# A third dense PSUM bank in the feed-forward part, three block sums and the samples' gating on GpSimd, and a recorder that knows the port shared with VectorE

## The chip, the cores and the metric

The kernel runs on one core of a Trainium2 chip. The core has a matrix engine (TensorE, PE in the profile), three engines for elementwise work (VectorE or DVE, ScalarE or ACT, GpSimd or POOL) and SyncE (SP), which here only starts transfers. They share an on-chip memory (SBUF); PE writes into eight banks of PSUM, which VectorE and ScalarE empty. The metric is the device time of one launch in microseconds (us), as the median over several runs.

## The reference

One layer of a decoder step for a prompt of 512 tokens and 8 x 4 sample tokens, which share all weights. D_MODEL is 1024, D_FF is 2816, everything is float32. The mixer and the cross attention come first; the part that the change touches is the feed-forward part and the last norm:

```
u = rmsnorm(x, norm_ffn)
ug = u @ w_gate
up = jnp.concatenate([conv_buf.astype(ug.dtype), ug], axis=1)
conv = conv_b + sum(conv_w[j] * up[:, j:j + T] for j in range(CONV_W))
x = x + (jax.nn.silu(conv) * (u @ w_up)) @ w_down
...
yp = rmsnorm(yp, norm_final)
ys = rmsnorm(ys, norm_final)
```

The prompt and the samples are two groups with conv states of their own; the kernel keeps their 512 + 32 = 544 tokens side by side as the columns of one matrix.

## The kernel before, in words

**Tiles.** Activations are kept transposed: 128 features on the partitions, 544 tokens along the row. D_MODEL is 8 such tiles (KT), D_FF is 22 (FT). A bank of PSUM holds 512 float32 numbers of a row, so every product is made in two halves of the tokens (CUTS: 256 and 288, LAST_CUTS: 288 and 256).

**Three products for one.** A float32 operand is split into a high part (rounded by a ScalarE cast to the fast matmul type) and a low part (what is left, a VectorE subtraction). A product is then high x high, high x low and low x high, three matmuls for each block of 128 x 128. Names that end in `h` and `l` are such parts: `wh` and `wl` of plain weights, `whg`, `wlg`, `whu`, `wlu` of gate and up weights, `wd_0h` and so on of down weights, `h16h` and `h16l` of hidden tile 16.

**The feed-forward part.** Tiles 0 to 3 of gate (`g`) and up (`u`) are plain products (`plain_tile`): 24 matmuls a half, into banks of the kind "dense" (`PD`, two of them). From tile 4 on, two tiles of one kind are made together by `Pair`, with a scheme that needs seven block products instead of eight. Its left factors are sums of weight blocks (A11, A12, S1 to S4, A22; S1 and S3 come from an accumulating transfer that GpSimd issues, S2 and S4 from VectorE). Its right factors are sums of blocks of the normed tokens: B11, B21, U, X, T, B22, V. These are made once, in `blocks(0)` and `blocks(1)`, each [128, 2, 272]: `norm` makes B11, B21, B12, B22 on VectorE, `combine` makes X = B12 - B22, T = B11 - B12, U = X - B11, V = B21 + U, `high` casts each, and `low` subtracts. The products of a pair go to three banks of the kind "aux" (`PX`, five): `ps_a`, `ps_d`, `ps_c`, followed by `g` or `u`. A unit is one pair of one kind; units 0 to 17 alternate gate and up for tiles 4, 6, ... 20.

**From gate and up to a hidden tile.** `conv` makes the three taps of the gate (ScalarE, then two VectorE operations, then Silu on ScalarE: `cv`) and copies the last columns away on GpSimd (`last`). `gated` multiplies up by it: `product` for the 512 prompt tokens on GpSimd, `product_s` for the 32 sample tokens on VectorE, then `high` and `low` split the result into `h..h` and `h..l`.

**Down.** The hidden tiles are taken in groups (DOWNS: 0 to 4, 4 to 8, 8 to 12, 12 to 16, 16 to 18), each 8 output tiles x 2 halves = 16 halves, 12 matmuls a half in a group of four blocks and 6 in the group of two. An entry says from which unit on the halves of a group may be placed, and how many go to each of the four places of a unit. Their bank is dense too (`ps_d`), and VectorE adds it to the residual `xr`. What is left goes behind the last unit. Tiles 18 to 21 (DOWN_LAST) make the last sixteen halves, `ps_dz`: first all eight tiles of the first tokens, then those of the others. Their weights are split into `wdhz` and `wdlz`.

**The end.** `final(c)` sums the squares over the features with two matmuls, makes 1/rms with Ln and Exp on ScalarE, and multiplies the residual by it and by the gain into `y`, on VectorE or (ON_POOL) on GpSimd, and sends it out. For the first half of tokens, ScalarE loads its table for Ln and Exp there, and the factor `r_fin` is in SBUF; for the second half VectorE reads it from a PSUM bank (`r_final`).

**The order of the work.** Nothing is issued as it is written. `Tape` records every operation as a `Step` with its engine, its estimated length, its tiles and what it depends on; `_Engine.take` holds the estimates. `order` then plays the five queues against each other with those lengths, takes for each free engine the ready step that is due first (`begin`), and issues in that order. It is a static order: on the chip every engine works its own queue strictly in it, and semaphores hold it where an input is late. `due` sets `begin` back from the matmuls that need a result; AHEAD says how many of the main PE steps before its own place a step may start at the earliest; `lead` and LEAD say how long before it is due. The profile calls nearly every instruction by the helper's line (606 for compute, 585 for a transfer), so it is read by the names of the tiles.

Of the kernel before, what the change touches and what calls it, by code (L numbers as in the profile page):

```python
# [10 lines left out]
F32 = mybir.dt.float32  # L11
F32R = mybir.dt.float32r
AF = mybir.ActivationFunctionType
# [20 lines left out]

PLAIN = 4

DOWNS = ((0, 4, 0, (1, 1, 1, 0)), (4, 8, 5, (1, 1, 1, 1)), (8, 12, 9, (1, 1, 1, 1)), (12, 16, 13, (1, 1, 1, 1)),
         (16, 18, 15, (1, 1, 1, 1)))
DOWN_LAST = (18, FT)
HT = N // 2  # L40
# [195 lines left out]
class Step:  # L236


    def __init__(self, engine, number, main):
        self.engine, self.number, self.main = engine, number, main  # L240
        self.calls, self.length, self.lag, self.bytes = [], 0.0, 0.2, 0
        self.deps, self.users, self.tiles = set(), [], set()
        self.gate, self.lead, self.after = None, None, set()

# [5 lines left out]
class Tape:  # L250
# [39 lines left out]
        dims = tuple(tuple(d) for d in ap.ap)  # L290
        return name, p0, p0 + dims[0][1], _bits(dims[1:]) << f0

    def put(self, engine, call, outs, ins, length, lag=None, size=0):
# [20 lines left out]
        cur.bytes += size  # L314
        if lag is not None:
            cur.lag = lag
        for ap, write in [(a, False) for a in ins] + [(a, True) for a in outs]:
            at = self.area(ap)
            if at is None:
                continue  # L320
            name, p0, p1, bits = at
            cur.tiles.add(name)
            kind = self.kinds.get(name)
            if kind in ("wraw", "whi", "wlo") and name not in self.seen:
                if kind in self.last:
                    cur.after.add(self.last[kind])
                self.last[kind] = cur
            found, keep = self.seen.setdefault(name, []), []
            for other in found:
                step, w, q0, q1, have = other  # L330
                if step is not cur and (write or w) and q0 < p1 and p0 < q1 and have & bits:
                    cur.deps.add(step)
                if not (write and p0 <= q0 and q1 <= p1 and have | bits == bits):
                    keep.append(other)
            keep.append((cur, write, p0, p1, bits))
            self.seen[name] = keep
            if write and engine == "PE":
                if name in self.writer and self.writer[name] is not cur:
                    cur.deps.add(self.writer[name])
                self.writer[name] = cur  # L340
        return None
# [40 lines left out]
    def due(self):  # L382

        for s in self.steps:
# [5 lines left out]
            if s.main:  # L390
                s.begin = s.est
            else:
                s.begin = s.soon + (self.SLACK if s.lead is None else 100.0)
                if s.engine in ("DVE", "ACT") and any(d.main for d in s.deps) and any(
                        self.kinds.get(n) in ("dense", "aux") for n in s.tiles):
                    s.begin = max(d.est + d.length for d in s.deps if d.main) + 1.0
            for d in s.deps:
                d.users.append(s)
# [24 lines left out]
    def order(self):  # L423
# [51 lines left out]
        def start(s):  # L475
# [11 lines left out]
                bus = max(bus, now) + s.bytes / 300e3  # L487
                s.end = bus + 2.0
            else:
                free[s.engine] = s.end = now + s.length  # L490
            if s.main:
                clock[:] = s.est, now
            for n in s.tiles:
# [23 lines left out]
        while todo:  # L517
# [4 lines left out]
            for e in ("SP", "ACT", "DVE", "POOL"):  # L522
                if free[e] <= now + 1e-9:
                    at = clock[0] + min(now - clock[1], 4.0)
                    can = [s for s in waiting[e] if s.ready <= now + 1e-9 and s.begin <= at + (s.lead or self.LEAD) and fits(s)]
                    if can:
                        start(min(can, key=lambda s: (s.begin, s.number)))
                        moved = True
            if free["PE"] <= now + 1e-9:
                can = [s for s in waiting["PE"] if s.ready <= now + 1e-9 and fits(s)]  # L530
# [34 lines left out]
class _Engine:  # L565
# [5 lines left out]
    def __getattr__(self, method):  # L571
# [3 lines left out]
        def take(*args, **kw):  # L575
# [6 lines left out]
            lag, size = 0.25, 0  # L582
            if method == "dma_start":
                size = 4 * int(np.prod(outs[0].shape))
                return tape.put(engine, lambda: call(*args, **kw), outs, ins, 0.1, 0.3, size)
# [15 lines left out]
            elif engine == "DVE":  # L601
                length = 0.13 + 0.00052 * n if method in ("tensor_scalar", "reciprocal") else 0.08 + 0.00105 * n
                length += 0.08 * ("accum_out" in kw)
            else:
                length = 0.15 + (0.0024 if method == "tensor_tensor" else 0.0009) * n
            return tape.put(engine, lambda: call(*args, **kw), outs, ins, length, lag, size)  # L606
        return take


# [1 line left out]
def tile_decoder_step(ctx: ExitStack, tc: tile.TileContext, xT, memT, kwT, vw, s0, conv_in, mkT, mv, vecs, cst,  # L611
# [23 lines left out]

    def PX(name):
        return tape.tile(psum, [128, 512], F32, tag="aux", name=name, bufs=5)

    def PDEC(name):
        return tape.tile(psum, [128, 512], F32, tag="dec", name=name, bufs=1)  # L640
# [1052 lines left out]

    dense_by_half(co_hl, KT, "co", co_evac, co_after)
    r_ffn, ux = ffn_in.r, ffn_in.hl
    tape.AHEAD = {"SP": 24, "ACT": 14, "DVE": 14, "POOL": 14, "PE": 14}
    ws.advance()
    ffn_in.rows(1)

# [47 lines left out]
    def conv(j, deps):  # L1747
# [13 lines left out]
                                               op0=ALU.mult, op1=ALU.add)  # L1761

        def gate():
            nc.scalar.activation(hid[j][:, :W], hid[j][:, :W], AF.Silu)

        job(ends, *deps)
        return job(gate, job(taps, job(first, *deps)))
# [1 line left out]
    def gated(j, deps):  # L1769
# [4 lines left out]

        def product_s():
            up, c = ups[j], hid[j]
            nc.vector.tensor_tensor(by_batch(up[:, SEQ:N]), by_batch(up[:, SEQ:N]), seg(c)[:, :, 0:4], op=ALU.mult)

        def high():
            hid[j] = R(f"h{j}h"), R(f"h{j}l")  # L1780
# [42 lines left out]
    def plain_half(w, xs, name, cut):  # L1823
# [2 lines left out]
        box = {}  # L1826

        def products():
            box["ps"] = PD(f"ps_{name}_{n0}")
            ws_, xs_ = w(), xs()  # L1830
            passes(box["ps"], ws_, xs_, n0, n, range(len(xs_)))

# [46 lines left out]


    tok, tok_low = {}, {}

    def blocks(kp):

# [12 lines left out]
                                               op0=ALU.mult, op1=ALU.mult)  # L1897

        def combine(name, a, b, op):
            nc.vector.tensor_tensor(place(name), tok[a, kp]["t"], tok[b, kp]["t"], op=op)  # L1900

        def split(name, part):
            tile = A if name in ("B11", "B21") or (name, part) == ("B22", "h") else B
# [4 lines left out]
            nc.scalar.copy(split(name, "h"), tok[name, kp]["t"])  # L1908

        def low(name):  # L1910
            nc.vector.tensor_tensor(split(name, "l"), tok[name, kp]["t"], tok[name, kp]["h"].bitcast(F32),
                                    op=ALU.subtract)

        for name in ("B12", "B22", "B11", "B21"):
# [164 lines left out]
    def last_half(m, c):  # L2079
        n0, n = LAST_CUTS[c]  # L2080
        cut = slice(n0, n0 + n)
        if m == 0 and c == 1:
            tape.gate_at = len(tape.mains) - 1
            nc.sync.dma_start(conv_out, last2)
            tape.gate_at = None
        ps = PD(f"ps_dz{m}_{c}")
        with tape.main():
            passes(ps, held[m], hs, n0, n, range(k))
        add_to(m)(ps, n0, n)
# [7 lines left out]
    def final(c):  # L2097
# [2 lines left out]
        ps = PX(f"psr_final{c}")  # L2100
        for i, sq in enumerate((ssq3.acc, last_sq)):
            nc.tensor.matmul(ps[:, :n], C("ones"), sq[:, cut], start=i == 0, stop=i == 1)
        with tape.together():
            if not c:
                nc.scalar.preload_act_table_set(LN_SET)
            nc.scalar.activation(r_fin[:, cut], ps[:, :n], AF.Ln, bias=eps, scale=1.0 / D)
        r = r_fin[:, cut]
        if c:

            r = PX("r_final")[:, :n]  # L2110
            nc.scalar.activation(r, r_fin[:, cut], AF.Exp, scale=-0.5)
# [99 lines left out]
```

## Time and profile before

| what | value |
| --- | --- |
| median of 3 runs | 842.91 us (842.23 to 843.27) |
| the profiled execution | 841.47 us |
| its span (first to last instruction) | 839.7 us |
| clock granted to TensorE, mean | 0.998 |
| TensorE busy | 821.3 us, 98% |
| VectorE busy | 592.0 us, 70% |
| ScalarE busy | 395.3 us, 47% |
| GpSimd busy | 182.9 us, 22% |

In the profile a row of a timeline gives the start, the length, the engine, the line, the operation, output <- inputs, the shape, and in brackets how long the engine had been idle and what ended that. A row of a group gives the count, the busy time, the mean of one in ns, and the idle time before the group's instructions. In a row of a stretch stand its bounds, its length, the busy time of PE, of PE's weight loads, of DVE, ACT and POOL with their instruction counts, the granted clock, the share of the DMA engines and GB/s. In a row by tile stand the shortest, middle and longest of the group in ns, and the first and last start.

The feed-forward part begins at about 450 us with the plain tiles; unit 0 begins at 500, the last product of a pair ends at 791, the `ps_dz` halves run from 804 to 831, and the last `y` is sent out at 836.

### The profile page before, as it was taken

To read this page: it belongs to the slowest core of one execution; us is meant where nothing else is said; L and a number is where in the kernel's file an instruction comes from. 1 tells how busy PE (TensorE), PEld (TensorE's weight loads), DVE (VectorE), ACT (ScalarE), POOL (GpSimd) and SP (SyncE) were. 2 spreads that over 40 slices of the span, in tenths; PEclk is the share of its full clock that TensorE was granted. 3 is DMA by queue.
4 is the path that set the end of the run, shared out by engine and by line. 5 is a ranking of instruction groups with operands and counts; after the bars stand their busy time and mean duration, and the time that the engine had idled before them with its cause. 6 is when DMAs were issued, how large, how long until landed. Compare 5 with 4: busy or idle time off the path is not lost.

```text
span 839.7 us, 18801 instructions
## 1 busy us (share of the span) xinstructions
PE 821.3 (98%) x7594; PEld 765.3 (91%) x7594; DVE 592.0 (70%) x1233; ACT 395.3 (47%) x792; POOL 182.9 (22%) x261
## 2 busy tenths in 40 slices
PE   9999999999999999999999999999999999999995
PEld 8989887878789879999789999999999999999995
DVE  6883725865888876564566997877877867767854
ACT  7422414543557454443445545555454545534623
POOL 1220000210210110222233252223213223232123
PEclk9999999999999999999999999999999999999999
DMA  9656895956833525161631246547455554564403
GB/s 321 221 140 191 260 334 190 301 168 221 291 111 104 181 82 179 59 216 36 223 113 51 76 124 155 139 123 193 132 124 141 157 148 124 156 161 115 134 1 107
DMA packets 90759, 132.32 MB, mean 158 GB/s; under 512 B 6064, under 2 KB 60080, under 8 KB 90544
## 3 DMA queue, kind: packets, MB, share of 16 engines
q1 hardware_dynamic: 84480, 120.69, 45.0%
q0 software_dynamic: 5184, 9.44, 7.0%
q8 instruction: 59, 0.97, 0.5%
q10 hardware_dynamic: 1008, 0.99, 0.3%
q14 instruction: 28, 0.23, 0.1%
HBM read 123.03 MB, written 8.07 MB: 156 GB/s over the span
## 4 chain that ended last, share of the span: by engine, by line
PE 84%; DVE 10%; issue 2%; DMA 1%; ACT 1%; POOL 1%; SPq 0%; DVEq 0%; POOLq 0%
PE ps_d L606 12%; PE ps_au L606 6%; PE ps_ag L606 6%; PE ps_wo L606 6%; PE ps_cg L606 3%; PE ps_cu L606 3%; PE ps_co L606 3%; PE ps_k L606 3%; PE ps_cq L606 3%; PE ps_hf L606 2%; PE ps_hq L606 2%; PE ps_v L606 2%; PE ps_hv L606 2%; PE ps_hg L606 2%; PE ps_dz L606 2%; PE ps_first L606 2%
## 5 line engine op out<-in xcount | busy, mean ns | idle before, releaser
L606 ACT CAST wh<-wr 128x1024 fp32r<-128x1024 f32 (+1 forms) x68 | 60.9, 908 | 109.3 <-PE ps_k L606 16.9
L606 DVE TENSOR_TENSOR wl<-wr,wh 128x1024 fp32r<-128x1024 f32 (+1 forms) x68 | 72.4, 1073 | 11.8 <-ACT wh L606 11.6
L606 POOL TENSOR_TENSOR up<-up,cv 128x512 f32<-128x512 f32 x22 | 34.1, 1552 | 165.0 <-ACT up L606 101.1
L606 POOL TENSOR_TENSOR hG<-hG,hf 128x256 f32<-128x256 f32 (+1 forms) x28 | 25.1, 895 | 189.0 <-DVE hf L606 127.8
L606 DVE TENSOR_TENSOR xr<-xr,ps_d 128x256 f32<-128x256 f32 x80 | 34.6, 433 | 23.8 <-PE ps_d L606 23.8
L606 DVE SCALAR_TENSOR_TENSOR cv<-ug,vec,cv 128x560 f32<-128x560 f32 x44 | 38.2, 868 | 0.2
L606 POOL COPY last<-ug 128x2 f32<-128x2 f32 (+1 forms) x44 | 19.9, 481 | 77.6 <-ACT ug L606 49.5
L606 POOL TENSOR_TENSOR acc_cx<-acc_cx,sq_cx 128x256 f32<-128x256 f32 (+1 forms) x14 | 11.9, 854 | 61.1 <-ACT sq_cx L606 61.0
L606 ACT ACTIVATE cv<-cv 128x560 f32<-128x560 f32 x22 | 14.8, 673 | 20.7 <-DVE cv L606 20.4
L606 PE MATMUL ps_co<-coh,wh 128*128 128x256 f32 (+1 forms) x64 | 19.0, 297 | 0.0
L606 ACT ACTIVATE cv<-ug,vec 128x560 f32<-128x560 f32 x22 | 18.8, 856 | 0.0
L606 ACT ACTIVATE P<-P,mx 128x128 f32<-128x128 f32 (+3 forms) x32 | 17.6, 551 | 2.7 <-DVE mx L606 2.7
L606 PE MATMUL ps_co<-coh,wl 128*128 128x256 f32 (+1 forms) x64 | 18.5, 288 | 0.0
L606 PE MATMUL ps_co<-col,wh 128*128 128x256 f32 (+1 forms) x64 | 18.4, 288 | 0.0
L606 DVE TENSOR_TENSOR xr<-xr,ps_wo 128x256 f32<-128x256 f32 (+1 forms) x16 | 6.8, 434 | 14.8 <-PE ps_wo L606 14.8
L606 DVE TENSOR_TENSOR xr<-xr,ps_dz 128x288 f32<-128x288 f32 (+1 forms) x16 | 7.0, 436 | 13.3 <-PE ps_dz L606 13.3
L606 PE MATMUL psd<-st,qbd_win 128*32 128x224 f32 x256 | 16.0, 359 | 0.0
L606 POOL TENSOR_TENSOR acc_ux<-acc_ux,sq_ux 128x256 f32<-128x256 f32 (+1 forms) x14 | 10.8, 771 | 21.3 <-ACT sq_ux L606 21.3
L606 ACT COPY keptru<-ps_au 128x272 f32<-128x272 f32 x9 | 3.5, 386 | 25.1 <-PE ps_au L606 25.1
L606 PE MATMUL psdo<-st,dpt 128*32 128x256 f32 x224 | 15.2, 385 | 0.0
L606 ACT ACT_TABLE_LOAD x11 | 14.1, 1283 | 2.3 <-issue 2.1
L606 DVE TENSOR_TENSOR hf<-hf 128x256 f32<-128x256 f32 (+1 forms) x28 | 11.9, 425 | 4.7 <-POOL hG L606 4.4
(2652 smaller groups left out, 3580.6 us busy)
## 6 DMA issues: line engine op xcount, KB each, us to landing
st<-in_kwT SPq DMA_DIRECT2D x32, 448.0 KB, 5.5
st<-in_vw SPq DMA_DIRECT2D x28, 512.0 KB, 5.2
wr<-in_w_in SPq DMA_DIRECT2D x25, 512.0 KB, 5.4
wd<-in_w_down SPq DMA_DIRECT2D x32, 256.0 KB, 3.8
wrg<-in_w_gate SPq DMA_DIRECT2D x9, 512.0 KB, 4.4
wru<-in_w_up SPq DMA_DIRECT2D x9, 512.0 KB, 5.8
st<-in_mkT SPq DMA_DIRECT2D x8, 512.0 KB, 5.2
wr<-in_w_out SPq DMA_DIRECT2D x8, 512.0 KB, 4.1
```

Source lines behind the costliest of these rows:

```text
L606: return tape.put(engine, lambda: call(*args, **kw), outs, ins, length, lag, size)
```

## The change

- `PF` takes the place of `PD` for plain halves, down halves and the last halves: every third of them goes to the bank of the kind "dec" (one bank, used before by the attention over the caches). `due` treats that kind as it treats dense and aux.
- The first down group is placed from unit 1 on with four halves a unit, before from unit 0 with three.
- `product_s` runs on GpSimd.
- The sums T and V, and the low parts of T, V and B22, are made on GpSimd, for both halves of the features: ten instructions of 128 x 544.
- The table for Ln and Exp is loaded together with the Silu of tile 21, and the first `final` reads its factor from PSUM too.
- In the recorder, VectorE steps of the operations `tensor_scalar` and `scalar_tensor_tensor` without a PSUM operand are marked `port`; in `order` such a step lasts until GpSimd is free and then its own length, and while GpSimd is busy it is ranked as if due 2 us later. The estimated lengths of GpSimd operations change. AHEAD in the feed-forward part grows from 24, 14, 14, 14 (SP, ACT, DVE, POOL) to 40, 30, 30, 30.

```diff
-DOWNS = ((0, 4, 0, (1, 1, 1, 0)), (4, 8, 5, (1, 1, 1, 1)), (8, 12, 9, (1, 1, 1, 1)), (12, 16, 13, (1, 1, 1, 1)),
+DOWNS = ((0, 4, 1, (1, 1, 1, 1)), (4, 8, 5, (1, 1, 1, 1)), (8, 12, 9, (1, 1, 1, 1)), (12, 16, 13, (1, 1, 1, 1)),
          (16, 18, 15, (1, 1, 1, 1)))
...
-                        self.kinds.get(n) in ("dense", "aux") for n in s.tiles):
+                        self.kinds.get(n) in ("dense", "aux", "dec") for n in s.tiles):
...
-                free[s.engine] = s.end = now + s.length
+                held_up = max(0.0, free["POOL"] - now) if s.port else 0.0
+                free[s.engine] = s.end = now + held_up + s.length
...
-                        start(min(can, key=lambda s: (s.begin, s.number)))
+                        busy = free["POOL"] > now + 0.1
+                        start(min(can, key=lambda s: (s.begin + 2.0 * (s.port and busy), s.number)))
...
+                port = method in ("tensor_scalar", "scalar_tensor_tensor") and not any(
+                    tape.kinds.get(a.tensor.name) in ("dense", "aux", "dec") for a in aps)
             else:
-                length = 0.15 + (0.0024 if method == "tensor_tensor" else 0.0009) * n
-            return tape.put(engine, lambda: call(*args, **kw), outs, ins, length, lag, size)
+                length = {"tensor_tensor": 0.2 + 0.0026 * n, "memset": 0.15 + 0.0007 * n,
+                          "tensor_scalar": 0.2 + 0.0036 * n}.get(method, 0.45 + 0.0009 * n)
+            return tape.put(engine, lambda: call(*args, **kw), outs, ins, length, lag, size, port)
...
+    def PF(name):
+
+        turn[0] += 1
+        return PDEC(name) if turn[0] % 3 == 0 else PD(name)
+
+    turn = [0]
...
-    tape.AHEAD = {"SP": 24, "ACT": 14, "DVE": 14, "POOL": 14, "PE": 14}
+    tape.AHEAD = {"SP": 40, "ACT": 30, "DVE": 30, "POOL": 30, "PE": 14}
...
         def gate():
-            nc.scalar.activation(hid[j][:, :W], hid[j][:, :W], AF.Silu)
+            with tape.together():
+                nc.scalar.activation(hid[j][:, :W], hid[j][:, :W], AF.Silu)
+                if j == FT - 1:
+                    nc.scalar.preload_act_table_set(LN_SET)
...
-            nc.vector.tensor_tensor(by_batch(up[:, SEQ:N]), by_batch(up[:, SEQ:N]), seg(c)[:, :, 0:4], op=ALU.mult)
+            nc.gpsimd.tensor_tensor(by_batch(up[:, SEQ:N]), by_batch(up[:, SEQ:N]), seg(c)[:, :, 0:4], op=ALU.mult)
...
-            box["ps"] = PD(f"ps_{name}_{n0}")
+            box["ps"] = PF(f"ps_{name}_{n0}")
...
+    ON_GPSIMD = ('T', 'V', 'B22')
...
-            nc.vector.tensor_tensor(place(name), tok[a, kp]["t"], tok[b, kp]["t"], op=op)
+            on = nc.gpsimd if name in ON_GPSIMD else nc.vector
+            on.tensor_tensor(place(name), tok[a, kp]["t"], tok[b, kp]["t"], op=op)
...
-            nc.vector.tensor_tensor(split(name, "l"), tok[name, kp]["t"], tok[name, kp]["h"].bitcast(F32),
+            (nc.gpsimd if name in ON_GPSIMD else nc.vector).tensor_tensor(split(name, "l"), tok[name, kp]["t"], tok[name, kp]["h"].bitcast(F32),
                                     op=ALU.subtract)
...
-        ps = PD(f"ps_dz{m}_{c}")
+        ps = PF(f"ps_dz{m}_{c}")
...
-        with tape.together():
-            if not c:
-                nc.scalar.preload_act_table_set(LN_SET)
-            nc.scalar.activation(r_fin[:, cut], ps[:, :n], AF.Ln, bias=eps, scale=1.0 / D)
-        r = r_fin[:, cut]
-        if c:
-
-            r = PX("r_final")[:, :n]
-            nc.scalar.activation(r, r_fin[:, cut], AF.Exp, scale=-0.5)
+        nc.scalar.activation(r_fin[:, cut], ps[:, :n], AF.Ln, bias=eps, scale=1.0 / D)
+
+        r = PX(f"r_final{c}")[:, :n]
+        nc.scalar.activation(r, r_fin[:, cut], AF.Exp, scale=-0.5)
         nc.scalar.activation(r_fin[:, cut], r_fin[:, cut], AF.Exp, scale=-0.5)
```

More of the change, by code (lines that the diff above doesn't have):

```diff
@@ L240, in __init__ @@
         self.engine, self.number, self.main = engine, number, main
-        self.calls, self.length, self.lag, self.bytes = [], 0.0, 0.2, 0
+        self.calls, self.length, self.lag, self.bytes, self.port = [], 0.0, 0.2, 0, False
         self.deps, self.users, self.tiles = set(), [], set()
@@ L291, in area, with put @@
         return name, p0, p0 + dims[0][1], _bits(dims[1:]) << f0
-    def put(self, engine, call, outs, ins, length, lag=None, size=0):
+    def put(self, engine, call, outs, ins, length, lag=None, size=0, port=False):
         main = self.in_main and engine == "PE"
@@ L314, in put @@
         cur.bytes += size
+        cur.port |= port
         if lag is not None:
@@ L581, in take @@
             n = max([int(np.prod(a.shape[1:])) for a in aps] + [1])
-            lag, size = 0.25, 0
+            lag, size, port = 0.25, 0, False
             if method == "dma_start":
```

## The prediction

> **What bounds the kernel.** I read the page first (busy shares), then the waits of TensorE, then busy time by stretch, and last the timeline of each engine around the places where TensorE stood still. TensorE (PE) is busy for 98% of the span, so what a change to the other engines can give is the time in which PE waits.
>
> ```profile
> span 839.7 us, 18801 instructions
> PE 821.3 (98%) x7594; PEld 765.3 (91%) x7594; DVE 592.0 (70%) x1233; ACT 395.3 (47%) x792; POOL 182.9 (22%) x261
> ```
>
> Busy time by stretch (us since the start; the first number after the bounds is the length) shows where those waits lie in the feed-forward part.
>
> ```profile
> 457.00:514.00 57.00, 54.55 (x431) 53.99 (x430) 53.90 (x94) 29.87 (x45) 19.51 (x24) 1.00 0.45 124
> 514.00:789.00 275.00, 275.00 (x2194) 275.00 (x2193) 205.16 (x361) 138.88 (x265) 72.69 (x118) 1.00 0.55 144
> 789.00:804.00 15.00, 13.01 (x91) 11.46 (x89) 14.22 (x31) 7.89 (x16) 2.91 (x4) 1.00 0.00 1
> 821.00:831.00 10.00, 8.56 (x67) 7.95 (x65) 6.03 (x11) 4.74 (x10) 6.31 (x8) 1.00 0.30 102
> ```
>
> From 514 to 789 PE never stops: nothing is to be had there. VectorE (DVE, the third busy number) is nearly full in 457 to 514 (53.9 of 57) and 789 to 804 (14.2 of 15). The matmuls at which PE had stood, with the idle time before each and what ended it, are these; the rows without a bracket bound a stretch.
>
> ```profile
> 484.94 0.37 PE L606 MATMUL ps_u<-ux0h,wh 128*128 128x288 f32 x1 [1.16 <-DVE ug L606]
> 505.16 0.38 PE L606 MATMUL ps_d<-h3h,wd_0h 128*128 128x256 f32 x1 [0.67 <-ACT h3h L606]
> 506.15 0.38 PE L606 MATMUL ps_d<-h3l,wd_0h 128*128 128x256 f32 x1 [0.61 <-DVE h3l L606]
> 792.51 0.29 PE L606 MATMUL ps_d<-h17h,wd_2l 128*128 128x288 f32 x1
> 804.02 0.40 PE L606 MATMUL ps_dz<-h18h,wdhz 128*128 128x288 f32 x1
> 827.91 0.39 PE L606 MATMUL ps_dz<-h18h,wdhz 128*128 128x256 f32 x1 [1.44 <-DVE xr L606]
> ```
>
> Between 792.64 and 804.02 lie ten halves of the group of two blocks (16, 18). The chain of waits gives what a half takes when nothing holds it:
>
> ```profile
> 783.81 0.71 PE ps_d L606 x6
> 789.03 0.81 PE ps_d L606 x6
> ```
>
> Ten of them are 5 x (0.71 + 0.81) = 7.6 us against 11.4 us taken, so 3.8 us are lost. With 1.16, 1.28 and 1.44 from the brackets, 7.7 us is all that PE loses where the change works.
>
> **The change part by part.**
>
> *Third dense bank* (PF). It adds no instruction. The waits at 484.94 and 827.91 are for one of two banks to be emptied by DVE. A plain half is 24 matmuls, twice a 12-matmul half of 1.42 or 1.62 (double the rows above), so about 3 us of room is added in the first case and 1.42 us in the second. Value at 484.94: -1.2 (bounds -1.2 and 0, if DVE is late by more than a bank). Late next there is the split of the plain weights, behind the same DVE.
>
> *The end* (table load beside the last Silu, first r in PSUM).
>
> ```profile
> 822.17 1.28 ACT L606 ACT_TABLE_LOAD   x1
> 824.48 3.05 DVE L606 SCALAR_TENSOR_TENSOR y<-xr,vec,r_fin 128x288 f32<-128x288 f32 x3 [0.39 <-ACT r_fin L606]
> 827.45 0.41 DVE L606 TENSOR_TENSOR xr<-xr,ps_dz 128x256 f32<-128x256 f32 x1
> L606 DVE SCALAR_TENSOR_TENSOR y<-xr,vec,r_fin x5: 505/972/1170, 824.5 to 828.2; 128x288 f32<-128x288 f32 x5
> L606 DVE SCALAR_TENSOR_TENSOR y<-xr,vec,r_final x6: 475/476/480, 833.7 to 835.7; 128x256 f32<-128x256 f32 x6
> ```
>
> The addition that frees PE's bank stood behind three y products of 3.05 us. The load of 1.28 us moves to the Silu of tile 21, where ScalarE has room (7.89 busy of 15), so Ln and y begin about 1.2 us sooner. With r in PSUM a y takes about 0.5 us, as the second half's do, instead of 0.97. One more Exp on ScalarE (0.4) is hidden. The PE wait of 1.44 goes, by the bank or by the shorter queue; what follows PE's last matmul is unchanged. Value -1.5, bounds -0.5 (another addition is late) and -2.0 (the later additions gain too).
>
> *Samples' gating on GpSimd* (product_s).
>
> ```profile
> L606 DVE TENSOR_TENSOR up<-up,cv x22: 176/186/1322, 470.2 to 796.9; 128x32 f32<-128x32 f32 x22
> L606 POOL TENSOR_TENSOR up<-up,cv x22: 1278/1517/2522, 468.6 to 796.7; 128x512 f32<-128x512 f32 x22
> 808.58 0.81 POOL L606 TENSOR_TENSOR acc_final<-acc_final,sq_final 128x288 f32<-128x288 f32 x1 [10.43 <-ACT sq_final L606]
> ```
>
> On GpSimd a product costs about (1.28 - 0.81) / 224 = 2.1 ns a column, so 32 columns are estimated at 0.26 us, 22 of them 5.8. It now stands behind the product of 512 on one queue, and the ScalarE cast of the hidden tile waits for both: 0.26 us more in that chain, and nothing for PE, since no half waited for a hidden tile from 514 to 789. DVE is rid of 22 instructions; where one came out at 1.3 us it had been held until the GpSimd product ended, and the next DVE product from SBUF can be held in its place. Value alone 0 (bounds -0.5 and +0.5).
>
> *The last two-block group.* DVE in 789 to 804:
>
> ```profile
> L606 DVE TENSOR_TENSOR wdlz<-wdz,wdhz 128x512 fp32r<-128x512 f32 x8 | 5.5, 681 | 0.0
> L606 DVE TENSOR_TENSOR xr<-xr,ps_d 128x288 f32<-128x288 f32 (+1 forms) x12 | 5.1, 428 | 0.8 <-PE ps_d L606 0.8
> L606 DVE TENSOR_TENSOR up<-up,cv 128x32 f32<-128x32 f32 x2 | 2.0, 984 | 0.0
> ```
>
> 2.0 us go with the samples' gating, the third bank lets an addition be a half later, DOWNS leaves eight halves behind the last product instead of ten, and the larger AHEAD (30 for ACT and DVE, 40 for SP) lets the eight wdlz splits, 5.5 us, begin before this stretch, where DVE has 70 us of 275 free. Their loads on SP and casts on ScalarE go with them; they hold tiles longer, which I price at 0 while work tiles are left. Without the splits and the gating DVE has 6.7 us to do in 15. Value -2.8, bounds -3.8 (all) and 0 (DVE still bounds). I choose nearer the first because 7.5 of DVE's 14.2 us can leave.
>
> *First down group from unit 1.* The three halves of unit 0 move to later units, which have four each; loads, casts, splits and additions go with them. PE work is the same. The wait for h3, 1.28 us, goes: value -1.3 (bounds -1.3 and 0). But unit 0 loses 4.5 us of cover (1.42 + 1.62 + 1.42), within which its weights were made ready. This price is joined to the next.
>
> *Block sums T, V and the lows of T, V, B22 on GpSimd.* Ten DVE instructions of 0.72 go (one pair shown); ten GpSimd ones of 1.28 + 32 x 0.0021 = 1.35 us (estimated) come, 13.5 us, in the stretch where DVE is full.
>
> ```profile
> L606 DVE TENSOR_TENSOR T<-B,B x2: 712/714/715, 487.5 to 488.1; 128x544 f32<-128x544 f32 x2
> L606 POOL TENSOR_TENSOR up<-up,cv 128x512 f32<-128x512 f32 x4 | 6.1, 1532 | 24.3 <-ACT cv L606 21.9 <-DVE up L606 2.5
> 458.93 0.91 DVE L606 SCALAR_TENSOR_TENSOR B<-xr,vec,r_ux 128x272 f32<-128x272 f32 x2
> 468.35 1.97 DVE L606 SCALAR_TENSOR_TENSOR B<-xr,vec,r_ux 128x272 f32<-128x272 f32 x2
> 482.40 1.32 DVE L606 TENSOR_TENSOR up<-up,cv 128x32 f32<-128x32 f32 x1
> 457.35 1.23 DVE L606 TENSOR_TENSOR wl<-wr,wh 128x1024 fp32r<-128x1024 f32 x1 [3.65 <-ACT wh L606]
> 495.42 1.70 DVE L606 TENSOR_TENSOR wlg<-wrg,whg 128x1024 fp32r<-128x1024 f32 x1
> ```
>
> DVE work on SBUF does not run beside a GpSimd product: two B norms take 1.97 instead of 0.91, a product of 32 columns 1.32 instead of 0.18, a split 1.70 instead of 1.23. So four products (6.1 us) held DVE for 1.06 + 1.14 + 0.47 = 2.7 us, 0.44 us per us. After the change PE needs 57 - 2.4 - 4.5 = 50.1 us for this stretch. DVE needs 53.9 - 7.2 (blocks) - 1.9 (gating) - 2 (additions and splits of the moved halves) = 42.8, which leaves 7.3. GpSimd adds 13.5 + 1.0 = 14.5 us; at 0.44 that holds DVE for 6.4 and just fits, at 1 it is 7.2 too much. Price 0 to +7.2; I take +2, near the measured ratio, because the sums can come in a burst.
>
> The Trainium skill, "SBUF — State Buffer", section "Who interferes with whom", says that a DVE instruction with two SBUF inputs contends with a GpSimd one that reads SBUF, and that the first to issue blocks the other wholly. The trace agrees (1.32 against 0.18), and it is a plain tensor-tensor product that was held; the recorder's new port mark leaves those out. By that rule alone, each sum holding DVE to its end, the price is the upper end, +7.2.
>
> *Recorder* (held_up, GpSimd lengths, port). No instruction of its own, but it reorders queues over the whole program: 0, bounds -1.5 and +1.5, of the size of the single waits above.
>
> **Sum.** -1.2 - 1.5 - 2.8 - 1.3 + 2.0 = -4.8 us. The profiled execution took 841.47 (its span and 1.77 around it), 1.44 below the median of 842.91; against it the sum is 836.7, on the median's scale 838.1.
>
> **Rivals.** *GpSimd holds DVE (slower).* The price is +7.2, and unit 0, without cover, waits for one sum more, since its accumulating load is issued from the same GpSimd queue:
>
> ```profile
> 497.83 1.03 POOL L585 DMA_DIRECT2D S1g<-in_w_gate  x1
> 502.55 0.69 DVE L606 TENSOR_TENSOR S2g<-S1g,wrg 128x512 f32<-128x512 f32 x1 [1.14 <-DMA S1g<-in_w_gate]
> ```
>
> It landed 4.7 us after the issue; behind one sum it is 1.35 later. -6.8 + 7.2 + 1.35 = +1.8: 844.7. It decides from a price of 6.8 on, a hold of (7.3 + 6.8 - 1.35) / 14.5 = 0.88 us per us. For it speaks that DVE is full and the recorder does not see products held; against it, that DVE's evacuations from PSUM run on.
>
> *All waits go.* The sums hide: -7.7, 835.2. For it: each wait has its own remedy. Against: DVE's spare is what holds take.
>
> *The last group stays DVE-bound.* Only the samples' gating leaves: -0.9 in place of -2.8, 840.0.
>
> **How the numbers follow.** My forecast 0.48, all waits go 0.12, last group bound 0.13, GpSimd holds DVE 0.22, no net change 0.05. Within 0.2% (841.2 to 844.6) is about what this measurement can't tell from nothing. Faster: 0.48 + 0.12 + 0.10 = 0.70; slower 0.22; same 0.08. The range, 834.5 to 845.5, runs from all waits gone to the slower rival with some reordering; the forecast's own is 836 to 840.
>
> **What would show it.** Right: no PE wait on DVE near 828, no table load there, y of both halves near 0.5 us; eight halves in about 7 us before dz; no wait for h3. For the block sums: DVE busy in the plain tiles and unit 0, and PE waits there for wl, S2g or a bank; over 6.8 us of them makes the prediction wrong, as would PE waits at 514 to 789 for hidden tiles or weights.

## The result, and the profile after

| what | before | after |
| --- | --- | --- |
| median of 7 runs each, in turns | 843.27 us (840.77 to 844.88) | 846.43 us (845.72 to 847.5) |
| ratio of the times, 95% interval | | 1.0041 (1.0027 to 1.0056) |
| the profiled execution | 841.47 us | 845.8 us |
| its span | 839.7 us | 843.6 us |

The change makes the kernel 0.4% slower. The forecast was 838.1 us, with a range of 834.5 to 845.5: the time lies above both. The page of the kernel after, with the group of the table loads, and then the first of the stretches shown of before:

```profile
span 843.6 us, 18802 instructions
PE 819.0 (97%) x7594; PEld 766.1 (91%) x7594; DVE 593.9 (70%) x1201; ACT 403.6 (48%) x798; POOL 207.2 (25%) x293
L612 ACT ACT_TABLE_LOAD x16 | 20.5, 1283 | 2.4 <-issue 2.2
```

```profile
457.00:514.00 57.00, 51.43 (x405) 50.57 (x404) 52.75 (x71) 28.92 (x42) 38.63 (x37) 1.00 0.39 108
```

PE has the same 7594 matmuls, so what counts is again where it stands still. From 457 to 514 it is busy for 51.43 us (before 54.55), while GpSimd works 38.63 (before 19.51). From 514 to 789 it never stops, as before. ScalarE loads a function table 16 times, before 11 times. The timeline of PE after: its waits from 457 on, and three rows without a bracket that bound the stages (the last product of a pair, the first and the last matmul of `ps_dz`).

```profile
481.68 0.39 PE L612 MATMUL ps_u<-ux0h,wl 128*128 128x256 f32 x1 [0.30 <-DVE wl L612]
490.11 0.39 PE L612 MATMUL ps_g<-ux0h,wl 128*128 128x256 f32 x1 [2.16 <-DVE wl L612]
507.21 0.40 PE L612 MATMUL ps_ag<-Uh,S2g4h 128*128 128x272 f32 x1 [2.05 <-ACT keptg L612]
511.55 0.40 PE L612 MATMUL ps_ag<-Th,S1g4h 128*128 128x272 f32 x1 [1.06 <-ACT keptg L612]
795.91 0.28 PE L612 MATMUL ps_cu<-Vh,A22u20l 128*128 128x272 f32 x1
801.31 0.36 PE L612 MATMUL ps_d<-h16h,wd_5h 128*128 128x256 f32 x1 [2.12 <-DVE xr L612]
805.90 0.30 PE L612 MATMUL ps_dz<-h18h,wdhz 128*128 128x288 f32 x1
828.92 0.39 PE L612 MATMUL ps_dz<-h18h,wdhz 128*128 128x256 f32 x1 [0.66 <-DVE xr L612]
831.74 0.28 PE L612 MATMUL ps_dz<-h21h,wdlz 128*128 128x256 f32 x1
833.35 0.70 PE L612 MATMUL psr_final<-acc_final,cs 128*128 128x256 f32 x2 [1.34 <-DVE acc_final L612]
```

The two bounds of before that the prediction did not show:

```profile
791.03 0.29 PE L606 MATMUL ps_cu<-Vh,A22u20l 128*128 128x272 f32 x1
830.73 0.28 PE L606 MATMUL ps_dz<-h21h,wdlz 128*128 128x256 f32 x1
```

Behind the last product lie twelve halves of the two-block group before (72 matmuls) and ten after (60), so 0.71 + 0.81 = 1.52 us of PE work has moved ahead of that bound. With it taken out, the span of 839.7 against 843.6 is split thus:

| stage | before, us | after, us | difference |
| --- | --- | --- | --- |
| to the last product of a pair | 791.03 | 795.91 - 1.52 | +3.4 |
| from there to `ps_dz` | 12.99 - 1.52 | 9.99 | -1.5 |
| `ps_dz` | 26.71 | 25.84 | -0.9 |
| behind the last matmul of `ps_dz` | 8.97 | 11.86 | +2.9 |

So two stages lost what the other two gained, and more. The waits for a bank at 484.94 and for `h3` are gone, as forecast. In their place stand waits for `wl` and `keptg`, one of 2.12 us in the last group, and a longer end. ScalarE's timeline shows what both of the latter have in common:

```profile
795.92 2.57 ACT L612 ACT_TABLE_LOAD   x2
798.51 0.67 ACT L612 ACTIVATE cv<-cv 128x560 f32<-128x560 f32 x1
799.08 0.39 ACT L612 CAST wd_7h<-wd 128x256 fp32r<-128x256 f32 x1
824.04 1.28 ACT L612 ACT_TABLE_LOAD   x1
825.85 1.28 ACT L612 ACT_TABLE_LOAD   x1
834.10 1.28 ACT L612 ACT_TABLE_LOAD   x1
835.88 1.28 ACT L612 ACT_TABLE_LOAD   x1
```

Two loads stand back to back between the last two Silus. The static order issued tile 21's Silu, with its load for Ln and Exp, ahead of tile 20's. Tile 20's Silu then needs its own table again, and nothing loads the other one in advance any more: each `final` loads twice, once ahead of Ln and once ahead of Exp. The cast of `wd_7h` stands behind the first two, and VectorE behind the cast:

```profile
799.50 1.30 DVE L612 TENSOR_TENSOR wd_7l<-wd,wd_7h 128x256 fp32r<-128x256 f32 x1 [1.88 <-ACT wd_7h L612]
800.73 0.44 DVE L612 TENSOR_TENSOR xr<-xr,ps_d 128x288 f32<-128x288 f32 x1
```

The addition that empties PE's bank is queued behind that split; hence the 2.12 us at 801.31. At the end, the two loads at 834.10 and 835.88 take 2.57 us; the first lies in part beside the matmuls that sum the squares (until 834.83), so from `sq_last` to `r_final` the kernel after takes 1.8 us more than e1_silu_order below, which has no loads there.

For the block sums, GpSimd's groups in 450 to 500 give the ten instructions (each name twice), and the two timelines show a stretch of them beside VectorE:

```profile
L612 POOL TENSOR_TENSOR B22l<-B,B22h 128x544 fp32r<-128x544 f32 x2 | 4.2, 2100 | 0.0
L612 POOL TENSOR_TENSOR T<-B,B 128x544 f32<-128x544 f32 x2 | 3.7, 1844 | 5.8 <-PE ps_g L612 4.6 <-DVE B L612 1.2
L612 POOL TENSOR_TENSOR Vl<-V,Vh 128x544 fp32r<-128x544 f32 x2 | 3.6, 1811 | 0.4 <-ACT Vh L612 0.4
L612 POOL TENSOR_TENSOR V<-B,U 128x544 f32<-128x544 f32 x2 | 3.6, 1798 | 2.4 <-DVE B L612 1.9 <-PE ps_g L612 0.5
L612 POOL TENSOR_TENSOR Tl<-T,Th 128x544 fp32r<-128x544 f32 x2 | 3.4, 1712 | 0.0
```

```profile
484.77 1.79 POOL L612 TENSOR_TENSOR V<-B,U 128x544 f32<-128x544 f32 x1 [1.93 <-DVE B L612]
486.53 2.45 POOL L612 TENSOR_TENSOR up<-up,cv 128x512 f32<-128x512 f32 x2
485.68 1.47 DVE L612 TENSOR_TENSOR Ul<-U,Uh 128x544 fp32r<-128x544 f32 x1
487.07 1.79 DVE L612 TENSOR_TENSOR B21l<-B,B21h 128x544 fp32r<-128x544 f32 x1
```

The ten take 18.5 us, where 13.5 was estimated. `Ul` starts at 485.68 and ends 0.6 us after `V` has ended at 486.56; `B21l` starts at 487.07 and ends within 0.1 us of the end, at 488.98, of GpSimd's pair of gating products. Each takes about 0.7 us elsewhere. The two holds, 0.76 and 1.07, make up most of the 2.16 us for which PE then waits for `wl`, the next split in VectorE's queue.

### The profile page after: what moved, and what is told of

Read it like the earlier page. It is cut to its first block, busy times and chain, and to the rows that moved or that the text cites. A ratio compares the mean times of both kernels' runs of the same rounds, so it can differ in the third digit from the quotient of the medians.

```text
span 843.6 us, 18802 instructions
## 1 busy us (share of the span) xinstructions
PE 819.0 (97%) x7594; PEld 766.1 (91%) x7594; DVE 593.9 (70%) x1201; ACT 403.6 (48%) x798; POOL 207.2 (25%) x293
## 4 chain that ended last, share of the span: by engine, by line
PE 81%; DVE 11%; ACT 3%; issue 2%; DMA 2%; POOL 1%; SPq 0%; DVEq 0%; POOLq 0%; ACTq 0%
PE ps_d L612 12%; PE ps_ag L612 6%; PE ps_wo L612 6%; PE ps_au L612 6%; PE ps_hv L612 3%; PE ps_k L612 3%; PE ps_co L612 3%; PE ps_cq L612 3%; PE ps_cu L612 3%; PE ps_cg L612 3%; PE ps_v L612 3%; PE ps_hq L612 2%; PE ps_hg L612 2%; PE ps_dz L612 2%; PE ps_hf L612 2%
## 5 line engine op out<-in xcount | busy, mean ns | idle before, releaser
L612 POOL TENSOR_TENSOR up<-up,cv 128x512 f32<-128x512 f32 (+1 forms) x44 | 45.8, 1051 | 138.9 <-ACT cv L612 109.6
L612 POOL COPY last<-ug 128x16 f32<-128x16 f32 (+1 forms) x44 | 15.6, 402 | 72.2 <-ACT ug L612 57.5
L612 POOL COPY ug<-conv_state 128x16 f32<-128x16 f32 x22 | 17.1, 782 | 0.0
L612 ACT COPY keptu<-ps_au 128x272 f32<-128x272 f32 x18 | 7.0, 389 | 20.3 <-PE ps_au L612 19.6
L612 DVE TENSOR_TENSOR kq<-hq,hf 128x256 f32<-128x256 f32 (+1 forms) x28 | 15.3, 548 | 0.0
```

## The experiments

Two theories stood. The first: the misplaced load costs the last group and the end, and the sums on GpSimd cost the start, as two separate faults. The rival: one of them explains nearly all, and the rest comes from what moved with the reordering (down halves, AHEAD, gating). Ratios are to the kernel before, on the same chip; the rounds ran on different chips, so ratios compare better than medians. 0.1% is 0.84 us.

| run | median, us | ratio | 95% interval |
| --- | --- | --- | --- |
| after | 846.43 | 1.0041 | 1.0027 to 1.0056 |
| e1_silu_order | 840.57 | 0.9980 | 0.9966 to 0.9993 |
| e2_sums_on_dve | 844.27 | 1.0027 | 1.0012 to 1.0043 |
| e3_both | 837.77 | 0.9939 | 0.9923 to 0.9954 |
| e4_before_sums | 847.59 | 1.0059 | 1.0042 to 1.0076 |
| e5_old_downs | 842.17 | 1.0002 | 0.9985 to 1.0020 |
| e6_bank_alone | 841.22 | 0.9990 | 0.9974 to 1.0005 |
| e7_early_sums_load | 838.41 | 0.9964 | 0.9952 to 0.9977 |
| e8_dead_sums | 854.87 | 1.0154 | 1.0126 to 1.0182 |
| e9_dead_sums_early | 852.01 | 1.0103 | 1.0078 to 1.0128 |
| e10_port_for_all | 841.91 | 0.9980 | 0.9966 to 0.9993 |
| e11_old_ahead | 838.31 | 0.9945 | 0.9924 to 0.9966 |
| e12_gating_on_dve | 840.38 | 0.9969 | 0.9957 to 0.9981 |

**The order of the last two Silus** (the kernel after, with one dependency more).

```diff
+    silus = {}
...
                 if j == FT - 1:
                     nc.scalar.preload_act_table_set(LN_SET)
+                    tape.cur.after.add(silus[FT - 2])
+                silus[j] = tape.cur
```

> The changed kernel with one order added: the Silu of tile 21 (with the table load behind it) is issued after the Silu of tile 20. On ScalarE's queue the two Silus change places and five table loads go; nothing else moves. Theory A (the misplaced load is half of the loss): the two loads of 1.28 us behind the last matmul go, 2.6 us, and r of the first half is ready some 2.6 us sooner, so the waits of 0.66 and 1.34 us behind it shrink: 3 to 4.5 us faster than the changed kernel, about 842.5. Theory B (the loss lies in the block sums alone): the loads only replace other waiting at the end, under 1 us.

ScalarE's order now differs from that of the kernel after in the two Silus, the casts of h20 and h21 that follow them, and five loads that are gone. Its timeline, and PE's three bounds:

```profile
795.82 1.24 ACT L612 ACTIVATE cv<-cv 128x560 f32<-128x560 f32 x2 [1.83 <-DVE cv L612]
797.08 1.28 ACT L612 ACT_TABLE_LOAD   x1
```

```profile
795.26 0.28 PE L612 MATMUL ps_cu<-Vh,A22u20l 128*128 128x272 f32 x1
803.10 0.40 PE L612 MATMUL ps_dz<-h18h,wdhz 128*128 128x288 f32 x1
828.12 0.28 PE L612 MATMUL ps_dz<-h21h,wdlz 128*128 128x256 f32 x1
```

The time falls by 0.6%, some 5 us, and the kernel is now faster than before. From the last product to `ps_dz` it takes 7.84 us: ten halves at full pace are 7.6. `ps_dz` takes 25.02 (after 25.84), and what lies behind it 9.7 (after 11.9). The gain is larger than expected, since the wait of 2.12 in the last group, which the expectation left out, went with the loads.

**The sums back on VectorE** (the kernel after, and the same with the Silus in order).

```diff
-    ON_GPSIMD = ('T', 'V', 'B22')
+    ON_GPSIMD = ()
```

> The changed kernel with the sums T and V and the lows of T, V and B22 back on VectorE; the misplaced table load stays. Theory A (GpSimd sums hold VectorE): the waits of PE for wl at 481 and 490 (0.3 and 2.2 us) go, and some of the 3.1 us in unit 0: 2.5 to 4 us faster than the changed kernel, about 843. Rival (unit 0 lost its cover of three down halves): the waits for wl go, but unit 0 waits as long or longer, since VectorE has 7 us more to do: within 1 us.

> Both of these edits. If the two causes add up, the sum of the two gains: 6 to 8 us faster than the changed kernel, 838 to 840, which is 3 to 5 us faster than the kernel before. If they overlap, about 842.

Alone the edit gives 1.2 us (1.0041 to 1.0027), less than expected and not clear of noise, as the intervals overlap; with the Silus in order 3.4 by the ratios, 2.8 by the medians. The intervals are too wide to say that the two differ. The waits for `wl` are gone in both, and one for `keptg` of 2.8 us at unit 0 is left. With both faults undone the kernel is 0.6% faster than before, the fastest by its ratio of all that were run (e11_old_ahead can't be told from it). PE's timeline of e3_both, and the cause of the wait on ScalarE:

```profile
504.28 0.59 PE L612 MATMUL ps_ag<-Uh,S2g4h 128*128 128x272 f32 x1 [2.82 <-ACT keptg L612]
794.47 0.29 PE L612 MATMUL ps_cu<-Vh,A22u20l 128*128 128x272 f32 x1
802.19 0.40 PE L612 MATMUL ps_dz<-h18h,wdhz 128*128 128x288 f32 x1
827.22 0.28 PE L612 MATMUL ps_dz<-h21h,wdlz 128*128 128x256 f32 x1
```

```profile
502.38 0.62 ACT L612 CAST S3g4h<-S3g 128x512 fp32r<-128x512 f32 x1 [2.09 <-DMA S3g<-in_w_gate]
503.85 0.38 ACT L612 COPY keptg<-ps_ag 128x272 f32<-128x272 f32 x1
```

`keptg`, which empties the bank, is queued behind a cast that waits for S3g to land. The stages of the three kernels against before, worked out as above, show where each fault cost (each is one execution; those of e1_silu_order and e3_both hold a stretch at half clock, told in the last section):

| stage | after | e1_silu_order | e3_both |
| --- | --- | --- | --- |
| to the last product of a pair | +3.4 | +2.7 | +1.9 |
| to `ps_dz` | -1.5 | -3.6 | -3.8 |
| `ps_dz` | -0.9 | -1.7 | -1.7 |
| behind it | +2.9 | +0.7 | -0.1 |
| span | +3.9 | -1.9 | -3.6 |

**The sums alone, on the kernel before.** Here only T, V and the lows of T, V and B22 move to GpSimd.

> The kernel before with only the sums T and V and the lows of T, V and B22 moved to GpSimd. If the sums hold VectorE: PE waits for plain weights or banks between 457 and 500, 2 to 5 us slower than before. If the freed 7.2 us of VectorE outweigh it: 0 to 2 us faster.

The cost is 5.0 us (0.59%), with no other part of the change. PE waits 1.56 and 1.28 us for a bank (`up`, `ug`) at 478.79 and 486.69, and 3.40 for `h3l` at 510.05:

```profile
510.05 0.58 PE L606 MATMUL ps_d<-h3l,wd_0h 128*128 128x256 f32 x1 [3.40 <-DVE h3l L606]
```

With it comes a stretch at half clock (0.50 from 508.4 to 515.1), so the 5.0 us are not waiting alone. This settles that the sums on GpSimd cost time by themselves.

**Ten dead sums.** Do they cost through GpSimd's use of the port, or because they make a chain longer? The kernel before keeps all its sums on VectorE, and GpSimd adds `T`, `V` or `B` to itself into a tile that nothing reads, ten times. In the first version these stood as jobs of their own:

> The kernel before with ten more additions of 128x544 on GpSimd, whose results nothing reads; VectorE keeps all its own sums, so only the time for which GpSimd holds what both need is added, at the places where T, V and B22 are ready. Theory (GpSimd holds VectorE): PE waits for banks and plain weights between 457 and 514, 4 to 8 us slower than before, at least as slow as e4. Rival (in e4 the sums themselves came late, or the recorder's order was worse): within 1 us of before.

The recorder put all ten behind everything else (834 to 849 us), so this run only has a longer end, and says nothing on the question. It gives the duration with no VectorE work to share with. In the second version each is issued with VectorE's own low part of that name; they run from 487 to 514, where the moved sums of e4_before_sums began at 473:

> The kernel before with ten more additions of 128x544 on GpSimd, each issued where T, V or the low of B22 stands (in e8 they were ordered to the end of the program); nothing reads them, VectorE keeps all its own sums. Theory (GpSimd holds VectorE while it adds): VectorE's own operations from SBUF come out up to 1.1 us longer between 475 and 514, and PE waits for banks, weights or h3: 3 to 7 us slower than before, as slow as e4 (+5.0). Rival (e4's loss was the order or the sums coming late): within 1 us of before.

A row by tile of the first, one of the second, and from the second's timelines a row of VectorE, one of PE and one of GpSimd:

```profile
L606 POOL TENSOR_TENSOR dead<-V x4: 1091/1091/1091, 840.9 to 847.9; 128x544 f32<-128x544 f32 x4
```

```profile
L606 POOL TENSOR_TENSOR dead<-T x4: 1457/1490/2036, 487.7 to 493.5; 128x544 f32<-128x544 f32 x4
```

```profile
495.46 2.24 DVE L606 TENSOR_TENSOR B22l<-B,B22h 128x544 fp32r<-128x544 f32 x2
513.09 0.58 PE L606 MATMUL ps_d<-h3l,wd_0h 128*128 128x256 f32 x1 [4.72 <-DVE h3l L606]
502.19 1.02 POOL L585 DMA_DIRECT2D S1g<-in_w_gate  x1
```

Additions whose results nobody waits for cost 1.0%, some 9 us. So the price is not a chain through the sums. The same addition takes 1.09 us alone and 1.49 in the middle beside VectorE; a pair of VectorE subtractions of 0.7 each takes 2.24. Ahead of the first long wait of PE (3.00 us for `ug` at 499.45) VectorE is held and never idle: between 488 and 499 its rows for `Tl`, `cv`, `B22l` and `up` take 9.0 us, in the kernel before 4.6.

Two things besides the hold are in the 9 us. The dead sums stand in GpSimd's own queue as well: S1g's transfer, next behind one of them (501.16 + 1.09), is issued at 502.19, before at 497.83; VectorE waits 1.80 us for it, and `h3l`, the cause of the wait of 4.72, is queued behind. And after both waits PE runs at half clock (0.50 from 499 to 502.3 and from 512.6 to 519.3). The waits between 457 and 515 are 5.5 us longer than before (7.97 against 2.44); half pace over the 9 us of these two stretches in which PE works costs some 4.5 us more, an estimate. The shares of the hold and of the queue in the price were not separated.

**The down halves.** e3_both, with the first group placed from unit 0 again, as before:

```diff
-DOWNS = ((0, 4, 1, (1, 1, 1, 1)), ...
+DOWNS = ((0, 4, 0, (1, 1, 1, 0)), ...
```

> The kernel of e3 with the down groups placed as before (first group from unit 0, three halves a unit). If the halves of unit 0 were the cover that its weights need, the wait of 2.8 us at 504 goes; the wait for h3 (1.3 us) may come back, and ten halves stand behind the last product. Theory cover: 1 to 2.5 us faster than e3, about 836. Rival (first down halves wait for h3 whatever covers them): 0 to 2 us slower than e3, about 839.

It is 4.4 us slower by the medians, 5.3 by the ratios. The last group waits again (0.40 + 0.61 us), and the largest wait is:

```profile
507.64 0.58 PE L612 MATMUL ps_d<-h3h,wd_0h 128*128 128x256 f32 x1 [4.65 <-ACT h3h L612]
```

The wait for `keptg` is gone, but the halves in unit 0 wait for `h3` instead, and longer. So starting the group a unit later is worth more in this kernel than the 1.28 us forecast.

**The third bank alone**, on the kernel before (PF for PD, and the kind in `due`).

> The kernel before with the third dense bank alone. The prediction gave it the wait at 484.94 (1.2 us) and part of the last group's 3.8 and of the 1.44 at 828. Theory: 2 to 4 us faster than before, about 839.5, with no PE wait for a bank before 790 and a shorter stretch of d16. Rival (VectorE, not the bank, is late): within 1 us of before.

The bank waits at 484.94 and near 828 are gone, and the last group has one wait of 0.89 us instead of three. But `h3` is waited for longer (1.96 + 0.62) and `psr_final` waits 1.77 us for the sum of squares. The interval holds no change: by the stages, the bank gives 2.5 us in the last group (10.53 against 12.99) and 1.5 in `ps_dz` (25.23 against 26.71), and 1.1 and 1.9 are lost ahead of the last product of a pair and behind `ps_dz`. The next waits in line take most of what it gives.

**S3g earlier.** e3_both, with the accumulating transfer's lead 9 instead of 4 and its load's 8 instead of 3:

> The kernel of e3 with the accumulating loads S1 and S3 allowed 5 us earlier (lead 9 in place of 4, the load under it 8 in place of 3), so that on GpSimd's queue S3g of unit 0 stands before the gating products and not behind them. Theory (unit 0 waits because S3g lands at 502 and ScalarE's keptg copy stands behind its cast): the wait of 2.8 us at 504 goes or falls under 1 us, 1.5 to 3 us faster than e3, about 835.5, better than both kernels. Rival (VectorE is late in unit 0 anyway): the wait stays above 2 us under another name, within 0.7 us of e3.

Not better than e3_both. S3g is issued at 489.45 instead of 497.11, but `keptg` is still waited for, 1.92 us at 505.59, now behind a Silu:

```profile
504.59 0.67 ACT L612 ACTIVATE cv<-cv 128x560 f32<-128x560 f32 x1 [1.62 <-DVE cv L612]
```

The Silu waits for VectorE's taps, so in unit 0 VectorE is late with the transfer early as well.

**A recorder that knows the whole port.** e1_silu_order, with plain products marked too:

```diff
-                port = method in ("tensor_scalar", "scalar_tensor_tensor") and not any(
+                port = method in ("tensor_tensor", "tensor_scalar", "scalar_tensor_tensor") and not any(
```

> The kernel of e1 (sums on GpSimd, Silus in order) with the recorder's port mark also for VectorE's tensor-tensor operations without a PSUM operand. Theory (the recorder places sums where they hold VectorE since it does not see it): the waits for wl at 481 and 489 (2.5 us) go, 1 to 3 us faster than e1, about 838.5. Rival (what both need is too little in this stretch, whatever the order): the waits move, within 1 us of e1 or slower.

The time is that of e1_silu_order. Both waits for `wl` are gone, but the feed-forward part starts some 4 us later (the last `ps_co` matmul at 453.52 instead of 449.46), as the edit changes the order of the whole program. A better model helped at the place in question and cost as much elsewhere.

**AHEAD and the gating.** e3_both with the old AHEAD (24, 14, 14, 14), and e3_both with `product_s` back on VectorE:

> The kernel of e3 with AHEAD of the feed-forward part as before (24, 14, 14, 14). The prediction gave the larger AHEAD a part of the last group's 2.8 us, since the wdlz splits can leave that stretch. Theory: eight wdlz splits return to the stretch before dz and PE waits there 1 to 3 us: about 839.5. Rival (bank and gating do it alone): within 0.7 us of e3.

> The kernel of e3 with the samples' gating back on VectorE. The prediction priced the move alone at 0 (-0.5 to +0.5), with 2.0 us of VectorE in the last stretch. Theory (off the path): within 0.7 us of e3. Rival (a held product in front of an addition matters in the last stretch): 1 to 2 us slower than e3, with PE waits on xr near 797.

AHEAD makes no difference to the time that can be measured (0.5 us, within the intervals). In the trace it does: the eight `wdlz` splits stand among the last halves again (from 796.24 on; in e3_both all eight lie before 789), PE waits 0.76 and 0.87 us there, and from the last product to `ps_dz` it takes 9.83 us instead of 7.72. That execution took 839.6 us and the median is 838.31; that each execution loses the 2.1 us is not shown. The gating on VectorE costs 2.5 us by the ratios, and the same stage takes 10.03 us instead of 7.72. VectorE's row shows why:

```profile
796.42 1.25 DVE L612 TENSOR_TENSOR up<-up,cv 128x32 f32<-128x32 f32 x1
```

A product of 32 columns is held for over a microsecond, and the addition that frees PE's bank stands behind it: PE waits 1.91 us at 798.18, which e3_both doesn't.

## Why the prediction was wrong

Two steps failed: the end, where a gain of 1.5 us was forecast and the order of the Silus cost 5.1 (after against e1_silu_order), and the block sums, priced at 2 us and costing 5.0 on the kernel before. Term by term:

- **Third bank, -1.2: the wait right, the gain not shown.** The wait at 484.94 is gone in every kernel with the bank; alone, the bank changed the time by no more than the noise (e6_bank_alone). What is late next was named (the split of the plain weights behind VectorE), and it is what PE waits for after: 0.30 + 2.16 us.
- **The end, -1.5: this step failed.** It took for granted that the load comes behind the last Silu. Nothing orders tile 21's Silu behind tile 20's. `due` sets a step's begin back by its length, and the step joined with the load is the longer one; that this put it first is argued from the code, but that the order is the fault is shown by e1_silu_order, where one added dependency takes five loads away. The y products do take what was forecast, 0.48 in the middle:

```profile
L612 DVE SCALAR_TENSOR_TENSOR y<-xr,vec,r_final x11: 473/479/516, 827.6 to 839.6; 128x256 f32<-128x256 f32 x6, 128x288 f32<-128x288 f32 x5
```

  With the order mended, `ps_dz` and what lies behind it gain 1.0 us (e1_silu_order) to 1.8 (e3_both); as built they lose 2.0.
- **Samples' gating, 0 (from -0.5 to +0.5): mis-sized.** It is worth about -2.5 in e3_both, 2.3 of it in the last group. The cost on GpSimd was also too low:

```profile
L612 POOL TENSOR_TENSOR up<-up,cv 128x32 f32<-128x32 f32 x22 | 12.1, 549 | 99.0 <-ACT cv L612 99.0
```

  The estimate was 0.26 us each, the mean is 0.55; it is hidden. What counted was the held product ahead of an addition, which the prediction showed (1322 ns) and priced only as a share of VectorE's time.
- **The last two-block group, -2.8 (-3.8 to 0): right in kind, and eaten.** The stage gives -3.6 and -3.8 once the Silus are in order, the whole of what was lost there, and -1.5 as built, because of the wait behind the two loads. Counted from the last product, ten halves stay behind it after twelve, not eight after ten. The bank, the gating and the larger AHEAD all have a part: without the gating the stage is 2.3 us longer, without the larger AHEAD 2.1 (in the one execution profiled), and the bank alone gives 2.5.
- **First down group from unit 1, -1.3: right in sign, too small.** e5_old_downs puts it at 4 to 5 us in this kernel.
- **Block sums on GpSimd, +2 (0 to +7.2): mis-sized.** Measured: 5.0 us on the kernel before, 1.2 to 3.4 in the changed one. I took the hold at 0.44 us per us of GpSimd work from four products. The ten sums take 18.5 us instead of 13.5 (held by VectorE in their turn: 1.09 us is what a dead one takes alone), and they come close together: 457 to 491. The ten dead ones cost 9.0 us, about 0.8 per us of the 10.9 they take alone, with the delay in GpSimd's queue and the half clock in it. The rule of the Trainium skill that the prediction weighed ("SBUF — State Buffer", section "Who interferes with whom") put the price at the upper end; the runs lie between it and my value.
- **Recorder, 0:** not measured by itself. e10_port_for_all shows that an edit of this kind can shift 4 us from one part of the program to another, more than the 1.5 allowed.

Of the rivals, "GpSimd holds DVE" had the direction and one of the two causes. It named a late S1g too, which is not there: S1g is issued at 492.13, before at 497.83. What unit 0 waits for lies behind S3g (issued at 500.53, in e3_both at 497.11). It gave 844.7, and the other cause, the table loads, was in none of the rivals. The sum of -4.8 us is nearly what another kernel gained: e3_both, with the sums left where they were and the Silus in order, is 5.1 us faster than before by its ratio. That is chance: without the price of the sums the same terms forecast -6.8 for that kernel.

## What to carry to other kernels

Work that is joined to another step, such as a table load, needs a stated dependency on everything that must come before it; an automatic order that knows only data dependencies and lengths can put it where it is undone and repeated. Before work is moved from a full VectorE to an idle GpSimd, ask how long it holds VectorE there, and what it delays in GpSimd's own queue: here ten sums of 0.7 us moved off it cost 5 us net, and ten that it never did cost 9, while a 32-column product that had been held in front of a critical addition was well worth moving. Where a resource is added (a bank), look for the next wait in line, which may take most of the gain.

## What the runs showed of the hardware

**The granted clock halves after some waits of PE.** In e3_both the wait of 2.82 us is followed by matmuls at half pace. The stretch by its windows, with the granted clock as the third number from the end, and two successive rows of PE:

```profile
504.00:506.00 2.00, 1.72 (x7) 1.72 (x8) 2.00 (x4) 0.90 (x2) 0.41 (x1) 0.50 0.01 4
```

```profile
504.67 0.43 PE L612 MATMUL ps_ag<-Ul,S2g4h 128*128 128x272 f32 x1
504.90 0.43 PE L612 MATMUL ps_ag<-Uh,S2g4l 128*128 128x272 f32 x1
```

They start 0.23 us apart, where such matmuls start 0.125 apart at full clock. Up to 510.34 that makes some 25 of them, or about 2.5 us. The same happened after a wait of 2.15 us in e1_silu_order (half clock from 489.6 to 493.0) and one of 1.92 in e7_early_sums_load (506.7 to 510.1), but not after one of 2.16 in the kernel after, nor after the wait for `keptg` of 2.81 in e2_sums_on_dve. At the same place in the last group it followed a wait of 2.16 in e2_sums_on_dve and not one of 2.12 in the kernel after. The Trainium skill, "TensorE: Matmul & The Clock Gate", section "What's actually happening", tells of an activity window of some 3.4 us that runs freely, at half rate after an idle one. The length of the dips fits, 3.4 us in e1_silu_order and 6.8 in e3_both (503.5 to 510.3); that the waits here are shorter than such a window does not. So a wait can cost twice, and not in every execution (the mean granted clock of the five of e3_both lies between 0.993 and 0.998): one execution's stage times carry 2 to 3 us of uncertainty around such a wait, the +1.9 of e3_both above among them.

**Ln and Exp loaded a table each.** Without the load in advance, each `final` has two loads of 1.28 us, one ahead of Ln and one ahead of Exp, though one load serves both in the kernel before and in e1_silu_order. The Silu after the two loads started 0.02 us behind their end (795.92 + 2.57, 798.51).

**GpSimd is held by VectorE as well.** The same 128x544 addition took 1.09 us alone and 1.49 beside a full VectorE, and the sums of the kernel after, which read two tiles where a dead one reads one tile twice, 1.71 to 2.10 in the mean of each pair.
